# A hybrid decoder layer on one core: the sums of the first channel tile's weights made by adding DMAs, and their high and low parts made beside the output projection

## The chip, the core and the metric

The kernel runs on one core of one Trainium2 chip. The metric is the device time of one execution in microseconds. Before the change three executions took 1217.89, 1218.16 and 1218.32 us; their median is 1218.16 us.

A core has a matrix engine (PE, whose weight loads the profile shows apart as PEld), three engines for elementwise work (DVE, ACT, POOL), a queue that issues most transfers (SP), and 16 DMA engines that carry the transfers out. Each engine runs its own instructions in a fixed order and waits for others by semaphores.

## The reference

What is computed is one decoder layer over 1024 tokens of width 1024, in float32. Cut to its frame:

```
h   = x * (1 + sc1) + sh1                      # the condition c gives six rows: sh, sc, g, twice
fox = forgetting_attention(h @ w_in ...)       # 8 heads of 64, causal softmax with a forget-gate bias
ret = retention(h @ w_in ...)                  # 4 heads of 128, in chunks of 128
x   = layer_norm(ALPHA * x + g1 * (concat(fox, ret) @ w_out), ln1)
h   = x * (1 + sc2) + sh2
u   = causal_depthwise_conv(h @ w_up)          # w_up: 1024 x 5632, width-3 convolution
a, b = split(u)
y   = (gelu(a) * b) @ w_down                   # w_down: 2816 x 1024
x   = layer_norm(ALPHA * x + g2 * y, ln2)
```

## The kernel before

**Float32 by parts.** The matrix engine multiplies a rounded float32 form (fp32r in the profile). So each operand is split into a high part (a cast, on ACT) and a low part (the operand minus its high part, on DVE), and each product is three matmuls: high by high, high by low, low by high.

**The stages, in order of time.** The retention heads and their projections (to about 222 us), the values of the attention heads (to about 273 us), eight attention heads of eight query blocks each (to about 480 us), the output projection `op_mm` over eight tiles of 128 tokens with the first layer norm (to about 575 us), the up-projection with convolution and gate over 22 channel tiles `ff` (to about 1000 us), and the down-projection with the second layer norm.

**Seven products for eight.** The up-projection multiplies 2x2 blocks in Winograd's way: for each channel tile seven products `prod(ff, p)` of sums of weight blocks with sums of input blocks. With `a` and `b` the two weight tiles of channel tile `ff` (loaded by `w_load`, each 128 x 8 x 128, lower half `[0:4]` and upper half `[4:8]`), the weights of the products are: `a` itself (`wA`, products 1 and 2), `b_low + b_high` and that plus `a_low` (`wS`, products 5 and 6, from `w_s`), `a_low + b_low` and `b_high` (`wD`, products 7 and 4, from `w_d`), and `a_high` plus the second half of the `wS` sum (`wZ`, product 3, from `w_4`). The sums are four instructions on DVE (L1217, L1219, L1232, L1240). Then come the high parts on ACT (L1199, L1243) and the low parts on DVE (L1203, L1244). For `ff = 0` all this stands between the last tile of the output projection and the channel loop (L1375 to L1406).

**The inputs of the products** are made at the same place. `h2_turn` transposes each normed tile on PE and writes it to the tiles `hr` by ACT (L910). `h2_low` makes the sums of input blocks on DVE (L937 to L949). `h2_split` makes the parts `t1`, `t2`, `t3`, `t4` (in the profile `ht`; high on ACT L879, low on DVE L883).

**Parking.** During the attention heads `w_out` is split piece by piece: `park_load` loads 128 x 512 floats, `park_high` and `park_low` make the parts on ACT (L990) and DVE (L997), and `park_store` writes them to device memory (`wod`), from where `wo_load` brings them back. There are 16 pieces.

**Adding DMAs.** `add_to` issues on POOL's queue a transfer that adds its source to its destination in device memory. It makes sums for the down-projection during the channel loop. Its destinations are filled beforehand by plain copies within device memory, `down_base` (L1112), during the attention heads.

**What sets the order.** A planner orders the instructions of each engine ahead of time, by their place in the program and by when it reckons their operands and their buffers to be ready. An instruction that is ready in this reckoning goes ahead of an earlier one that is not. On the chip each engine then keeps that order and waits where an operand is late. `tc.issue_after(ins)` puts the instructions of its block that run on the engine of `ins` behind `ins` in that order; it does nothing to other engines. `pins` keeps instructions to be named so.

**Buffers.** On-chip tiles share slots by tag. Those that matter here: X has 16 slots of 4 KB per partition, S 3, R 4, and the small T 4. When the channel loop begins, X holds eight tiles `hr` and the eight tiles of the two inputs `11` and `21`. S holds the second half-tiles of the output projection (`so`) and the gate row `g_row`. Tiles of attention weights (`wqkr`, loaded by `fox_w` at L638 two heads ahead) are in R.

Of the kernel before, what the change touches and what calls it, by code (L numbers as in the profile page):

```python
# [8 lines left out]
F32 = mybir.dt.float32  # L9
F32R = mybir.dt.float32r  # L10
# [5 lines left out]
P = 128  # L16
S = 1024
# [6 lines left out]
NFF = DFF // P  # L24
# [7 lines left out]
def kernel(  # L32
# [23 lines left out]
    nc = tc.nc  # L56
# [10 lines left out]
    def slot(tag, shape, dtype, name, padded=None):  # L67
        return gp.tile(shape, dtype, tag=tag, bufs=NB[tag], name=name, padded_shape=padded)
# [714 lines left out]
    def fox_scores(h, i, T, beside=None):  # L783
        qh, ql, ks, nb = T["qh"], T["ql"], T["ks"], T["nb"]
        span = (i + 1) * P
        tag = "S" if i % 2 == 0 else "R" if h < FH - 1 else "VM"
        Ssb = slot(tag, [P, S], F32, f"S{h}_{i}")
        cuts = [(0, min(max(span, 256), 512))]
        if span > 512:
            cuts.append((512, max(span, 768)))  # L790
        mn = small([P, 1], f"mn{h}_{i}")
        qs = slice(i * P, (i + 1) * P)
        pt = bank2(f"ps{h}_{i}")
        for k0, k1 in cuts:
            last = k0 <= i * P < k1
            nc.tensor.matmul(pt[:, k0:k1], qh[:, qs], ks[:, k0:k1], start=True, stop=False)
            nc.tensor.matmul(pt[:, k0:k1], ql[:, qs], ks[:, k0:k1],
                             start=False, stop=not last)
            if last:
                nc.tensor.matmul(pt[:, i * P:(i + 1) * P], identb, maskb,  # L800
                                 start=False, stop=True)
        pins["min"] = nc.vector.tensor_tensor_reduce(  # L802
            out=Ssb[:, :span], in0=pt[:, :span], in1=nb[:, :span], scale=1.0, scalar=3e38,
            op0=ALU.add, op1=ALU.min, accum_out=mn,
        )
        if beside is not None:
            beside()
        den = small([P, 1], f"dn{h}_{i}")
        pins["exp"] = nc.scalar.activation(  # L809
            Ssb[:, :span], Ssb[:, :span], AF.Exp, scale=-1.0, bias=mn, accum_out=den,  # L810
        )
        nc.vector.reciprocal(den, den)  # L812
        nc.gpsimd.tensor_tensor(  # L813
            out=Ssb[:, :span], in0=Ssb[:, :span], in1=den.to_broadcast([P, span]),
            op=ALU.mult,
        )
        return Ssb
# [152 lines left out]
    def h2_split(key, sl):  # L970
        for c in range(2):
            top_hi(key, c, sl)
            low = top_lo(key, c, sl)
        return low
# [1 line left out]


    wod = [dp.tile([2, P, D], F32, tag=f"wod{m}", name=f"wod{m}") for m in range(ND)]
    PIECES = [(m, slice(n, n + 512)) for m in (4, 5, 6, 7, 0, 1, 2, 3) for n in (0, 512)]
    park, wo = {}, {}  # L980

    def park_load(k):
        if k < len(PIECES):
            m, sl = PIECES[k]
            park[k] = [tmp([P, 512], F32, f"park{k}_{u}") for u in range(2)]
            nc.sync.dma_start(park[k][1], w_out[m * P:(m + 1) * P, sl])

    def park_high(k):
        hi, raw = park[k]
        nc.scalar.copy(hi.bitcast(F32R), raw)  # L990

    def park_low(k):

        if k in park:
            hi, raw = park[k]
            with tc.issue_after(pins["min"].ins):
                nc.vector.tensor_tensor(out=raw.bitcast(F32R), in0=raw, in1=hi, op=ALU.subtract)  # L997

    def park_store(k):
        if k in park:  # L1000
            m, sl = PIECES[k]
            for u, t in enumerate(park.pop(k)):
                nc.sync.dma_start(wod[m][u][:, sl], t)

    def wo_load(m):
        wo[m] = []
# [53 lines left out]
    def op_mm(i, m4):  # L1060
        for n in range(2):
            op_half(i, m4, n)
# [29 lines left out]
    def op_end(i):  # L1092
        for n in range(2):
            op_sum(i, n)
        op_mean(i)
        op_norm(i)
# [8 lines left out]
    def add_to(dst, src):  # L1105
        return nc.gpsimd.dma_start(dst, src, accum_op=ALU.add, max_dma_last_dim=2048)  # L1106

    def down_base(m):
        for q, k in [divmod(v, NK) for v in range(m, 4 * NK, FH)]:
            t, n = ((0, 0), (1, 1), (1, 1), (1, 0))[q]  # L1110
            with tc.issue_after(pins["nb"].ins):
                nc.sync.dma_start(td[q, k], wdq[t, k][:, n * 512:(n + 1) * 512])  # L1112

    LAG = 3
    LOADS = {0: (4, 5), 1: (6, 7), 2: (0, 1), 3: (2, 3)}
    T = {0: fox_alloc(0)}
# [10 lines left out]

    for s_ in range(FH * NT + LAG + 1):
        h, i = divmod(s_, NT)
        if h < FH:  # L1130
            if i == 0:
                if h % 4 == 0:
                    for half in range(2):
                        mixF[h // 4, half] = slot("VM", [P, 2, 512], F32, f"mixF{h // 4}_{half}")
            if i == 3:
                w = nw
                if h + 1 < FH:
                    T[h + 1] = fox_alloc(h + 1)
            if i >= 3:
                proj(h, i)  # L1140
            k, late = divmod(s_ - 4, 3)
            Sb[s_] = fox_scores(h, i, T[h], (lambda: park_low(k - 1)) if late == 1 else None)
            if i == 4 and h + 2 < FH:
                nw = fox_w(h + 2)
            if i == 6:
                down_base(h)
            if late == 0 and k >= 0:
                park_load(k)
            if late == 1:
                park_store(k - 1)  # L1150
            if late == 2 and k in park:
                with tc.issue_after(pins["exp"].ins):
                    park_high(k)
        r = s_ - LAG - 1
        if r >= 0 and r % 2 == 1:
            fox_pv(r // NT, (r % NT) // 2)
        r = s_ - LAG
        if 0 <= r < FH * NT:
            fox_turn(r // NT, r % NT, Sb.pop(r))
        if h < FH and not (i >= 3):  # L1160
            proj(h, i)
        if h == FH - 1 and i == 0:
            for q in range(2):
                op_load(q)
            g_row = slot("S", [P, D], F32, "g_row0")
            nc.sync.dma_start(g_row, bcast_rows(gates[0], D))
        if h == FH - 1:
            for m in LOADS.get(i, ()):
                wo_load(m)
            if i in (2, 3):  # L1170
                op_split(i - 2, 1)
            if i >= NT - 2:
                op_half(0, 1, i - NT + 2)
        if s_ == FH * NT:
            for q in range(2):
                x_load(q)
                sos[q] = slot("X", [P, S], F32, f"so{q}")
        if s_ == FH * NT + 1:
            op_mm(1, 1)
            op_split(0, 0)  # L1180
# [9 lines left out]
    def w_load(ff, u):  # L1190
        if ff < NFF:
            t = slot("R", [P, ND, P], F32, f"w{'ab'[u]}{ff}")
            nc.sync.dma_start(t, w_up[u * NFF + ff])
            (ra, rb)[u][ff] = t
# [27 lines left out]
    def w_s(ff, tag="X"):  # L1222

        if ff < NFF:
            w_s_sums(ff)
            W[ff, 5], W[ff, 6] = w_split(rs[ff], tag, f"wS{ff}")

    def w_d(ff, tag="X"):

        if ff < NFF:  # L1230
            a, b = ra[ff], rb[ff]
            nc.vector.tensor_tensor(out=b[:, 0:4, :], in0=a[:, 0:4, :], in1=b[:, 0:4, :],  # L1232
                op=ALU.add)
            W[ff, 7], W[ff, 4] = w_split(b, tag, f"wD{ff}")
# [125 lines left out]


    for i in range(NT - 1):
        op_mm(i, 0)
        op_split(i + 1, 0)
        if i + 2 < NT:
            x_load(i + 2)
            op_load(i + 2)
            op_split(i + 2, 1)
        op_end(i)
        if i > 0:  # L1370
            h2_turn(i - 1)
            h2_low(i - 1)
            op_mm(i + 1, 1)

    w_load(0, 0)  # L1375
    w_load(0, 1)
    w_load(1, 0)
    with tc.issue_after(pins["norm"].ins):
        w_a(0, "VM")
# [10 lines left out]
    with tc.issue_after(pins["norm"].ins), tc.issue_after(pins["bias"].ins):  # L1390
        h2_split("t1", slice(0, 3 * P))
        up_12(0)
        w_s(0, "S")
        h2_turn(NT - 1)
        h2_low(NT - 1)
        for key in ("t2", "t1"):
            low = h2_split(key, slice(3 * P, 4 * P))
        up_65(0, 0)
        with tc.issue_after(low.ins):
            up_12(1)  # L1400
        w_d(0)
        h2_split("t3", slice(0, 4 * P))
        h2_split("t4", slice(0, 4 * P))
        w_4(0)
    w_load(1, 1)
    w_load(2, 0)  # L1406

    for ff in range(NFF):
        up_657(ff)
        w_s(ff + 1)  # L1410
        w_d(ff + 1)
        w_load(ff + 2, 1)
        if ff + 2 == NFF:
            w_4(ff + 1)
        if ff > 0:
            up_12(ff + 1)
        if ff + 2 < NFF:
            w_a(ff + 2)
        up_43(ff)
        if ff + 2 < NFF:  # L1420
            w_4(ff + 1)
        w_load(ff + 3, 0)
        geglu(ff)
# [312 lines left out]
```

## Time and profile before

| what | value |
|---|---|
| median of three executions | 1218.16 us |
| the profiled execution, its own time | 1220.08 us |
| its span, first to last instruction | 1218.4 us |
| granted clock of the matrix engine, mean | 0.998 |
| DVE busy, share of the span | 910.4 us, 75% |
| ACT busy, share of the span | 653.1 us, 54% |
| POOL busy, share of the span | 229.1 us, 19% |
| moved by DMA, mean | 178 GB/s |

A span is what one profiled execution shows from its first to its last instruction; 1.7 us of the execution lie around it. Times of day in the views are microseconds from the start of the span. Rows of a timeline read: start, length, engine, line, operation, output and inputs, count, and in brackets how long the engine sat idle before it and what ended that. Rows of a table by windows read: the window, its length, then for PE, PEld, DVE, ACT and POOL the busy time and the number of instructions, then the granted clock, the share of the DMA engines and GB/s.

### The profile page before, as it was taken

Reading aid. Unit: us, or ns where it says so; the run is one execution under the profiler, and the core shown is the slowest. Engines: PE = TensorE matmul, PEld = TensorE weight load, DVE = VectorE, ACT = ScalarE, POOL = GpSimd, SP = SyncE. Lnnn points to the kernel's source line nnn. Section 1 sums busy time; section 2 is a strip of 40 time slices with the busy share of each in tenths; the row PEclk is TensorE's granted clock in tenths of the full one; section 3 lists DMA queues with packets and bytes.
Section 4 is the critical chain, followed back from the end, with each engine's and each line's share of the span. In section 5 each row is a group of like instructions: output and inputs, shape, how many; then the busy total and the mean of one; then the engine's idle time right before and its main releaser. Section 6 shows DMA issues by size and latency. Waiting matters only on the chain.

```text
span 1218.4 us, 17192 instructions
## 1 busy us (share of the span) xinstructions
PE 1199.6 (98%) x6005; PEld 1002.2 (82%) x6005; DVE 910.4 (75%) x1757; ACT 653.1 (54%) x1201; POOL 229.1 (19%) x274
## 2 busy tenths in 40 slices
PE   8999999999999999999999999999999999999997
PEld 6788888998888888888888888888888878888885
DVE  7847747766788887456988778787787775876596
ACT  6635445346777776567754545445454554544452
POOL 0015335013323333000021323211100010000021
PEclk9999999999999999999999999999999999999999
DMA  9524444604575558223268887776454588966751
GB/s 357 226 87 123 138 154 135 205 29 147 167 238 169 185 189 335 95 75 117 87 177 208 191 220 187 173 188 175 141 138 130 154 250 270 331 216 199 260 178 69
DMA packets 94278, 216.56 MB, mean 178 GB/s; under 512 B 10784, under 2 KB 17136, under 8 KB 94192
## 3 DMA queue, kind: packets, MB, share of 16 engines
q1 hardware_dynamic: 81520, 192.40, 45.7%
q0 software_dynamic: 12672, 23.07, 11.8%
q8 instruction: 47, 0.77, 0.3%
q14 instruction: 39, 0.32, 0.1%
HBM read 173.45 MB, written 76.59 MB: 205 GB/s over the span
## 4 chain that ended last, share of the span: by engine, by line
PE 88%; DMA 5%; DVE 3%; ACT 2%; issue 1%; SPq 0%; DVEq 0%; ACTq 0%
PE rp L152 11%; PE dX L1477 10%; PE dZ L1477 7%; PE uX L1260 6%; PE uX L1259 6%; PE uX L1261 6%; PE uY L1261 5%; PE uY L1259 5%; PE uY L1260 5%; PE vp L152 4%; DMA ada<-in_ada_dram 3%; PE pv L851 3%; PE op L189 2%; PE op L191 2%; PE op L190 2%; PE pt L835 2%
## 5 line engine op out<-in xcount | busy, mean ns | idle before, releaser
L152 PE MATMUL rp<-wr,hhi 128*128 128x512 f32 x400 | 127.9, 401 | 0.0
L1454 ACT CAST dh<-dr 128x1024 fp32r<-128x1024 f32 x66 | 67.6, 1050 | 77.9 <-DMA dr<-td 31.7
L1466 DVE TENSOR_TENSOR dl<-dr,dh 128x1024 fp32r<-128x1024 f32 x66 | 80.1, 1237 | 37.5 <-ACT dh L1454 37.2
L813 POOL TENSOR_TENSOR S<-S,dn 128x128 f32<-128x128 f32 (+3 forms) x64 | 73.6, 1154 | 152.8 <-DVE dn L812 126.0
L1106 POOL DMA_DIRECT2D sd<-gd x22 | 18.1, 823 | 399.8 <-DMA sd<-y 233.3
L152 PEld LDWEIGHTS rp<-wr,hhi 128*128 128x128 f32 x400 | 71.6, 189 | 12.7
L152 PE MATMUL rp<-wr,hlo 128*128 128x512 f32 x200 | 78.6, 393 | 0.0
L1477 PE MATMUL dX<-dh 128*128 128x512 f32 x176 | 68.5, 389 | 0.0
L1477 PE MATMUL dX<-dl,dh 128*128 128x512 f32 x176 | 68.5, 389 | 0.0
L1477 PE MATMUL dX<-dh,dl 128*128 128x512 f32 x176 | 68.5, 389 | 0.0
L1274 ACT COPY u<-uX 128x512 f32<-128x512 f32 x44 | 25.7, 585 | 69.1 <-PE uX L1261 69.1
L152 DVE CUSTOM_DVE_ANT_0 ada<-ada,csb,bcol 128x1024 f32<-128x1024 f32 x46 | 60.1, 1309 | 3.5 <-DMA ada<-in_ada_dram 3.5
L842 DVE TENSOR_TENSOR pt<-pt,pt 128x512 fp32r<-128x512 f32 (+2 forms) x96 | 50.6, 549 | 10.7 <-ACT pt L841 9.2
L809 ACT ACTIVATE S<-S,mn 128x128 f32<-128x128 f32 (+3 forms) x64 | 49.9, 780 | 13.6 <-DVE mn L802 13.0
L765 PE MATMUL qk<-hhi,wqh 128*128 128x512 f32 x128 | 55.1, 430 | 0.0
L802 DVE CUSTOM_DVE_ANT_0 S<-ps,nb 128x128 f32<-128x128 f32 (+3 forms) x64 | 47.5, 742 | 6.1 <-PE ps L800 5.2
L841 ACT CAST pt<-pt 128x512 fp32r<-128x512 f32 (+2 forms) x96 | 43.9, 479 | 14.5 <-PE pt L835 13.6
L1477 PE MATMUL dZ<-dh 128*128 128x512 f32 x132 | 51.6, 391 | 0.0
L767 PE MATMUL qk<-hhi,wql 128*128 128x512 f32 x128 | 51.5, 402 | 0.0
L1477 PE MATMUL dZ<-dl,dh 128*128 128x512 f32 x132 | 51.4, 389 | 0.0
L1477 PE MATMUL dZ<-dh,dl 128*128 128x512 f32 x132 | 51.4, 389 | 0.0
L189 PE MATMUL op<-wo,mxs 128*128 128x512 f32 x128 | 51.1, 399 | 0.0
(1048 smaller groups left out, 3655.0 us busy)
## 6 DMA issues: line engine op xcount, KB each, us to landing
ada<-in_ada_dram SPq DMA_DIRECT2D x48, 512.0 KB, 3.8
td<-in_w_down_dram SPq DMA_DIRECT2D x44, 256.0 KB, 5.9
wa<-in_w_up_dram SPq DMA_DIRECT2D x22, 512.0 KB, 4.8
wb<-in_w_up_dram SPq DMA_DIRECT2D x22, 512.0 KB, 4.2
gd<-y SPq DMA_DIRECT2D x22, 512.0 KB, 3.2
sd<-y SPq DMA_DIRECT2D x44, 256.0 KB, 3.4
dr<-sd SPq DMA_DIRECT2D x44, 256.0 KB, 4.2
dr<-td SPq DMA_DIRECT2D x44, 256.0 KB, 4.5
```

The source lines that it names most:

```text
L152: order[key] = fn(*args, **kw)
L189: mm(pt, ahi, whi, start=start, stop=False)
L765: nc.tensor.matmul(pt, whi[:, j, :], hhi[j][:, sl], start=(j == 0), stop=False)
L767: nc.tensor.matmul(pt, wlo[:, j, :], hhi[j][:, sl], start=False, stop=(j == ND - 1))
L813: nc.gpsimd.tensor_tensor(out=Ssb[:, :span], in0=Ssb[:, :span], in1=den.to_broadcast([P, span]), op=ALU.mult,)
L842: nc.vector.tensor_tensor(out=dl, in0=src, in1=f(dh), op=ALU.subtract)
L1259: nc.tensor.matmul(pt, whi, bh, start=start, stop=False, skip_group_check=True)
L1260: nc.tensor.matmul(pt, whi, bl, start=False, stop=False, skip_group_check=True)
L1261: nc.tensor.matmul(pt, wlo, bh, start=False, stop=stop, skip_group_check=True)
L1454: nc.scalar.copy(hi, raw)
L1466: nc.vector.tensor_tensor(out=lo, in0=raw, in1=f(hi), op=ALU.subtract)
L1477: nc.tensor.matmul(pt, w_[:, 0, q], m_[:, 1, :], start=start and n_ == 0, stop=stop and n_ == 2, skip_group_check=True)
```

## The change

The weight sums of channel tile 0 are no longer made by `w_s(0)`, `w_d(0)` and `w_4(0)`. There are four steps in their place.

1. `up_base`, called in the fifth attention head at its third block, copies four half-tiles of `w_up` (128 x 512 floats each) to new tiles `usum` in device memory, by four transfers on SP's queue, behind the load of that head's bias row (`pins["nb"]`).
2. `up_adds`, called before the first product of the output projection, issues four adding DMAs on POOL, behind POOL's last product of the attention heads (`pins["pool"]`, L813). The third reads what the first made, the fourth what the third made.
3. Five more pieces are parked, one in each of the first five tiles of the output projection: the upper half of `b`, which needs no sum, and the four sums. Their high parts stand behind the norm of the next tile on ACT, their low parts behind its second sum on DVE. Both parts are stored to new tiles `upd`.
4. `up_parts` loads the parts where `w_s(0)`, `w_d(0)` and `w_4(0)` stood: two tiles of 512 KB in S (`wS0`), two of 512 KB in X (`wD0`), two of 256 KB in S (`wZ0`).

The load of the whole tile `b` of channel tile 0, `w_load(0, 1)`, falls away. The DVE instructions of `w_s(1)` are put behind the last low part of `t4`. The matmuls are the same.

```diff
@@ fox_scores
-        nc.gpsimd.tensor_tensor(
+        pins["pool"] = nc.gpsimd.tensor_tensor(
@@ parking
-    PIECES = [(m, slice(n, n + 512)) for m in (4, 5, 6, 7, 0, 1, 2, 3) for n in (0, 512)]
+    PIECES = [(w_out[m * P:(m + 1) * P, n:n + 512], [wod[m][u][:, n:n + 512] for u in range(2)])
+              for m in (4, 5, 6, 7, 0, 1, 2, 3) for n in (0, 512)]
...
-    def park_low(k):
+    def park_low(k, behind="min"):
...
@@ before the head loop
+    ua0, ub0 = [[w_up[u * NFF][:, k:k + 4, :] for k in (0, 4)] for u in range(2)]
+    usum = [dp.tile([P, 4, P], F32, tag=f"usum{k}", name=f"usum{k}") for k in range(4)]
...
+    NW = len(PIECES)
+    for n, src in ((3, ub0[1]), (0, usum[0]), (1, usum[1]), (2, usum[2]), (4, usum[3])):
+        PIECES.append((flat(src), [flat(upd[2 * (n // 2) + u][:, n % 2]) for u in range(2)]))
+
+    def up_base():
+        for k, src in ((0, ub0[0]), (1, ua0[0]), (2, ua0[0]), (3, ua0[1])):
+            with tc.issue_after(pins["nb"].ins):
+                nc.sync.dma_start(usum[k], src)
+
+    def up_adds():
+        for k, src in ((0, ub0[1]), (2, ub0[0]), (1, usum[0]), (3, usum[1])):
+            with tc.issue_after(pins["pool"].ins):
+                add_to(flat(usum[k]), flat(src))
+
+    def up_parts(n, tag, name):
+        out = []
+        for u, c in enumerate("hl"):
+            t = slot(tag, [P, 8 if n < 2 else 4, P], F32, f"{name}{c}")
+            nc.sync.dma_start(t, upd[2 * n + u].rearrange("p t k c -> p (t k) c"))
+            out.append(t.bitcast(F32R))
+        return [tuple(t[:, k:k + 4, :] for t in out) for k in ((0, 4) if n < 2 else (0,))]
@@ head loop
+            if (h, i) == (4, 2):
+                up_base()
-            if late == 0 and k >= 0:
+            if late == 0 and 0 <= k < NW:
                 park_load(k)
@@ output projection
     for i in range(NT - 1):
+        if i == 0:
+            up_adds()
+        park_load(NW + i)
         op_mm(i, 0)
...
         op_end(i)
+        if NW + i - 1 in park:
+            with tc.issue_after(pins["norm"].ins):
+                park_high(NW + i - 1)
+            park_low(NW + i - 1, "sum")
+            park_store(NW + i - 1)
...
-    w_load(0, 1)
...
-        w_s(0, "S")
+        W[0, 5], W[0, 6] = up_parts(0, "S", "wS0")
...
-        w_d(0)
+        W[0, 7], W[0, 4] = up_parts(1, "X", "wD0")
         h2_split("t3", slice(0, 4 * P))
-        h2_split("t4", slice(0, 4 * P))
-        w_4(0)
+        end = h2_split("t4", slice(0, 4 * P))
+        W[0, 3] = up_parts(2, "S", "wZ0")[0]
...
     for ff in range(NFF):
         up_657(ff)
-        w_s(ff + 1)
+        if ff == 0:
+            with tc.issue_after(end.ins):
+                w_s(ff + 1)
+        else:
+            w_s(ff + 1)
```

More of the change, by code (lines that the diff above doesn't have):

```diff
@@ L983, in park_load @@
         if k < len(PIECES):
-            m, sl = PIECES[k]
             park[k] = [tmp([P, 512], F32, f"park{k}_{u}") for u in range(2)]
-            nc.sync.dma_start(park[k][1], w_out[m * P:(m + 1) * P, sl])
+            nc.sync.dma_start(park[k][1], PIECES[k][0])
     def park_high(k):
@@ L990, in park_high @@
         nc.scalar.copy(hi.bitcast(F32R), raw)
-    def park_low(k):
+    def park_low(k, behind="min"):
         if k in park:
             hi, raw = park[k]
-            with tc.issue_after(pins["min"].ins):
+            with tc.issue_after(pins[behind].ins):
                 nc.vector.tensor_tensor(out=raw.bitcast(F32R), in0=raw, in1=hi, op=ALU.subtract)
@@ L1000, in park_store @@
         if k in park:
-            m, sl = PIECES[k]
-            for u, t in enumerate(park.pop(k)):
-                nc.sync.dma_start(wod[m][u][:, sl], t)
+            for dst, t in zip(PIECES[k][1], park.pop(k)):
+                nc.sync.dma_start(dst, t)
     def wo_load(m):
@@ L1112, in down_base @@
                 nc.sync.dma_start(td[q, k], wdq[t, k][:, n * 512:(n + 1) * 512])
+    ua0, ub0 = [[w_up[u * NFF][:, k:k + 4, :] for k in (0, 4)] for u in range(2)]
+    usum = [dp.tile([P, 4, P], F32, tag=f"usum{k}", name=f"usum{k}") for k in range(4)]
+    upd = [dp.tile([P, 2 if k < 2 else 1, 4, P], F32, tag=f"upd{k}_{u}", name=f"upd{k}_{u}")
+           for k in range(3) for u in range(2)]
+    NW = len(PIECES)
+    flat = lambda t: t.rearrange("p k c -> p (k c)")
+    for n, src in ((3, ub0[1]), (0, usum[0]), (1, usum[1]), (2, usum[2]), (4, usum[3])):
[15 more added lines that the diff above has]
+        return [tuple(t[:, k:k + 4, :] for t in out) for k in ((0, 4) if n < 2 else (0,))]
     LAG = 3
```

## The prediction

> **What bounds the kernel now.** I read the page first, for the busy shares and the chain that ended last.
>
> ```profile
> PE 1199.6 (98%) x6005; PEld 1002.2 (82%) x6005; DVE 910.4 (75%) x1757; ACT 653.1 (54%) x1201; POOL 229.1 (19%) x274
> ...
> PE 88%; DMA 5%; DVE 3%; ACT 2%; issue 1%; SPq 0%; DVEq 0%; ACTq 0%
> ```
>
> The matrix engine is busy for 98% of the span and carries 88% of the chain. The change leaves every matmul as it is, so it can gain only where PE stands still. Next I asked the table by windows around the place that the change empties, and the waits of PE from 500 to 610 us.
>
> ```profile
> 520.00:530.00 10.00, 10.00 (x50) 8.35 (x49) 4.46 (x11) 5.21 (x14) 0.00 (x0) 1.00 0.22 80
> ...
> 590.00:600.00 10.00, 9.10 (x51) 7.74 (x50) 9.85 (x14) 6.12 (x8) 0.00 (x0) 1.00 0.16 52
> 600.00:610.00 10.00, 10.00 (x45) 8.27 (x45) 10.00 (x12) 7.29 (x9) 0.00 (x0) 1.00 0.35 107
> ```
> ```profile
> PE uX L1260 <- DVE ht L883: 0.9, 1, 0.9
> ```
>
> Between 500 and 610 us PE waits once, 0.9 us, for DVE, and DVE is full there (9.85 of 10). PE's own timeline has the wait, and the chain has what stands before it.
>
> ```profile
> 592.76 0.28 PE L1261 MATMUL uY<-ht,wS0l 128*128 128x256 f32 x1
> 592.88 0.46 PE L1259 MATMUL uX<-ht,wD0h 128*128 128x512 f32 x1
> 594.24 0.50 PE L1260 MATMUL uX<-ht,wD0h 128*128 128x512 f32 x1 [0.90 <-DVE ht L883]
> 594.58 0.40 PE L1261 MATMUL uX<-ht,wD0l 128*128 128x512 f32 x1
> 594.81 0.39 PE L1259 MATMUL uX<-ht,wD0h 128*128 128x512 f32 x1
> ```
> ```profile
> 589.18 1.66 ACT ht L879 x3
> 590.84 0.96 ACT wD0h L1199
> 591.83 1.23 DVE wD0l L1203
> 593.05 1.15 DVE ht L883
> ```
>
> Matmuls of 512 columns start 0.23 us apart (594.58 to 594.81). From 592.88 to 594.24 are 1.36 us, so 1.13 are lost, and 0.11 more at the restart (594.24 to 594.58). **1.24 us is all that this place can give**: 0.1% of the time. The cause is as the change assumes: the low part of `t3` stands behind the split of `wD0`, ACT then DVE, and both go away.
>
> [...]
>
> **The change, part by part.** *Off DVE and ACT at the transition.*
>
> ```profile
> 580.25 0.69 DVE L1217 TENSOR_TENSOR ws<-wb 128x512 f32<-128x512 f32 x1
> ...
> 582.18 0.68 DVE L1240 TENSOR_TENSOR wa<-wa,ws 128x512 f32<-128x512 f32 x1
> ...
> 584.25 1.22 DVE L1203 TENSOR_TENSOR wS0l<-ws,wS0h 128x1024 fp32r<-128x1024 f32 x1
> ...
> 589.68 1.43 DVE L883 TENSOR_TENSOR ht<-hr,ht 128x256 fp32r<-128x256 f32 x4
> ...
> 595.24 0.68 DVE L1244 TENSOR_TENSOR wZ<-wa,wZ 128x512 fp32r<-128x512 f32 x1
> ```
> ```profile
> 582.71 1.05 ACT L1199 CAST wS0h<-ws 128x1024 fp32r<-128x1024 f32 x1
> 583.66 0.83 ACT L879 CAST ht<-hr 128x768 fp32r<-128x768 f32 x1
> 584.39 2.90 ACT L910 ACTIVATE hr<-nT,AB 128x128 f32<-128x128 f32 x8
> ```
>
> Four sums (0.69 each, the first and the last are shown), 1.22, 1.23 and 0.68 leave DVE: 5.9 us. ACT loses two casts of 1.05 and the half cast of `wZ`, some 2.6 us. The low part of `t3` then follows the four small `ht` (they end at 591.1) at once and, with 1.15 us, is out by 592.3, before PE asks. The wait for DVE goes. What is late next is the transfers that take its place.
>
> *`wD0` in X.* X is full with `hr` and the two inputs until the first small `ht` has read its `hr`: 589.68 plus a quarter of 1.43 is 590.04. Both loads of `wD0` stand behind such a release. It comes earlier by what leaves ACT ahead of the eight `hr` of 584.39, the cast of `wS0` (0.95 from start to start): about 589.1, and 589.4 for the second slot.
>
> ```profile
> so<-mixR SPq DMA_DIRECT2D x5, 256.0 KB, 2.8
> wb<-in_w_up_dram SPq DMA_DIRECT2D x2, 512.0 KB, 3.5
> ```
> ```profile
> DMA to landing us min/median/max: 3.4/4.7/9.1
> ```
>
> The first two rows are transfers of 480 to 600 us (KB each, median us to landing); the third is of all weight loads, L1193. With 3.5 us `wD0h` lands at 592.6 and `wD0l` at 592.9, or up to 0.8 later because the two share the engines (an estimate: half of the 1.7 us that 512 KB take at the 312 GB/s of a row below). PE asks for the high part at 592.88 and for the low one two matmuls later, at 593.33. So the new wait is 0 to 0.4 us with 3.5 us of landing, 0.9 to 1.6 with 4.7, and over 5 with 9.1. Traffic is low there (a share of 0.16), so I take the near rows: **0.3 us**. [...]
>
> *`wZ0` in S.* S has three slots for the four tiles of `wS0` and `wZ0`. The low part of `wZ0` must wait until PE has used `wS0`: 592.76 plus 0.28. With 2.8 us it lands at 595.9. PE asks for it after the twelve matmuls of product 7 (593.1 plus 12 x 0.23) and two of product 3, at 596.3. Product 4 cannot be pulled ahead, since DVE must first read the same bank. I take **0.1 us**, with bounds 0 and, at the 4.7 us of a weight load, 1.4. `wS0` itself takes the slots that the last squares and sums of the projection leave, ahead of the norm of the last tile, and costs nothing.
>
> *The adding DMAs* go to an engine with nothing to do: POOL ends its last product at 481.3 and is idle until the channel loop. How long an adding DMA takes is in the row of L1106.
>
> ```profile
> 479.40 1.90 POOL L813 TENSOR_TENSOR S<-S,dn 128x1024 f32<-128x1024 f32 x1 [1.72 <-DVE dn L812]
> ```
> ```profile
> DMA to landing us min/median/max: 4.0/6.0/11.7
> ```
>
> Three in a chain take 18 us at the median, 35 at most: done by 500 or 517. The sums are wanted one per tile of 48 matmuls (11 us), the first a tile after the projection begins, the last of the chain three tiles after that. Cost 0; were the first late by a tile, SP would hold up one `so` load.
>
> *Parking beside the projection.* Five casts and five subtractions, by the rows of the sixteen pieces of before:
>
> ```profile
> L990 ACT CAST park<-park x16: 603/607/632, 297.6 to 445.2; 128x512 fp32r<-128x512 f32 x16
> L997 DVE TENSOR_TENSOR park<-park,park x16: 679/690/1164, 301.1 to 449.6; 128x512 fp32r<-128x512 f32 x16
> ```
>
> That is 0.6 us of ACT and 0.7 of DVE in each of five tiles. PE covers both. The tightest tile is the fifth, where DVE also makes the first sums of input blocks:
>
> ```profile
> 546.79 1.25 ACT L1089 ACTIVATE acc<-acc,onm,ors 128x1024 f32<-128x1024 f32 x1 [1.63 <-DVE onm L1088]
> ```
> ```profile
> 550.51 1.04 PE L902 MATMUL nT<-ident,acc 128*128 128x128 f32 x8
> ```
>
> Its norm ends 2.5 us before PE turns the tile, and the added cast stands behind the norm, so it does not hold it. Behind the cast on ACT wait only casts for the next tile's products, which a pass of 24 matmuls (5.4 us) separates from PE. SP gets a load and two stores per tile; behind the stores stands the next `so` load, whose slot comes free only with the next tile's square, some 10 us later. Cost 0; without that cover 0.7 us per tile, 3.5 in all.
>
> *`up_base` in the heads.* Four transfers of 256 KB at 0.6 us of SP each, in the one stretch where SP and the DMA engines are full:
>
> ```profile
> 358.71 1.83 SPq L1112 DMA_DIRECT2D td<-in_w_down_dram  x3
> 360.65 0.52 SPq L638 DMA_DIRECT2D wqkr<-in_w_qk_dram  x1
> 361.22 0.43 SPq L986 DMA_DIRECT2D park<-in_w_out_dram  x1
> 366.48 0.33 SPq L1003 DMA_DIRECT2D wod<-park  x1
> ```
> ```profile
> 360.65 7.30 DMA wqkr<-in_w_qk_dram
> 367.97 1.06 ACT wqh L641
> ```
> ```profile
> 360.00:365.00 5.00, 5.00 (x34) 4.22 (x33) 4.54 (x10) 2.86 (x5) 0.00 (x0) 1.00 0.99 312
> ```
> ```profile
> 376.48 0.63 PE L835 MATMUL pt<-ident,S 128*128 128x128 f32 x4 [0.74 <-DVE ks L777]
> ```
>
> The bias row of the fifth head goes out before all this; the copies of `td` behind it come first, being earlier in the program. SP is then free from 361.65 to 366.48. There four issues of 0.6 us fit, and behind them wait only a store, a bias row for a later head and more copies. At that place I take **0.2 us** for their traffic (1 MB at 312 GB/s, 3.4 us of full DMA). The bounds are 0 and 3.4.
>
> **The sum** is -1.24 + 0.3 + 0.1 + 0.2 = -0.6 us: 1219.5 for the profiled execution's 1220.08, and 1217.6 against the median of 1218.16. A measurement of this kernel can tell about 0.2%, 2.4 us, from no change, and this is a quarter of that.
>
> **The rivals.** *The wait only changes its name.* Loads that can start only when a slot comes free land 4.7 us later, not 3.5: 1.2 us for `wD0`, up to 0.7 for `wZ0`, and the fox stretch as above. That gives back 1.2 to 1.9 for 1.24: 1218.2 to 1219.0. For it speaks that the slots are freed by the very chain that sets the wait; against it the low traffic. The change would then not do what it says.
>
> *Slower: `up_base` goes ahead of the weights of head 5.* `wqkr` at 360.65 waits for a slot, and copies from later in the program (three of them in the row) were let past it. Copies from device memory to device memory wait for no slot, so four more may pass if the planner saw SP idle there. Each puts 256 KB at 312 GB/s, 0.84 us, ahead of a load that ACT uses the moment it lands, and PE's 0.74 us at 376 lie on the chain behind it. The transition's own gain is 0.84 (1.24 less 0.3 and 0.1), so one passing eats it and the second makes the kernel slower. With all four it is 1217.3 + 3.4 = 1220.7, which alone can be measured. Against it: `wqkr` follows the sixth copy at once.
>
> [...]
>
> **How the numbers follow.** Forecast 0.57 (1216.9 to 1218.2). The wait renamed 0.17. `up_base` ahead 0.20, half of it beyond 0.2%. Room in PE, or a luckier order of the heads, 0.03. Another order of the heads or of SP in the projection that costs over 2.4 us, 0.03. So faster by over 0.2%: 0.03; slower: 0.10 + 0.03 = 0.13; within: 0.84. The range goes from 1216.7, where the transition gives everything (1216.9, less 0.2 for the spread of the runs), to 1220.9, all four copies ahead and the same spread.
>
> **What would show it.** Right: PE's wait for DVE `ht` in 590 to 600 us is gone and at most 0.6 us of waits for transfers `wD0` or `wZ0` stand there; PE is 9.4 or more of 10; no PE wait appears in 500 to 580; `wqkr` of head 5 still leaves before the four copies. Wrong: a wait of ACT for `wqkr` longer than 0.8 us with PE idle behind it, waits of ACT for `so` in the projection, or PE waiting over 1.2 us at the transition.

## The result, and the profile after

The changed kernel takes **1221.62 us** (median of nine executions, 1220.42 to 1223.19) against 1218.09 us of the kernel before, run beside it (1217.51 to 1219.65). The ratio is 1.0024 with a 95% interval of 1.0015 to 1.0032: slower by some 3 us. In a later comparison with the kernel before (1218.75 us) it was 1220.44 us, ratio 1.0015 (1.0002 to 1.0029). The profiled execution took 1223.19 us, its span is 1221.5 us. The prediction was 1217.6 us, with a range up to 1220.9.

The place that the change was made for did get better. The table by windows of the changed kernel (columns as before: window, length, busy time and count of PE, PEld, DVE, ACT, POOL, clock, DMA share, GB/s):

```profile
590.00:600.00 10.00, 9.87 (x54) 8.13 (x53) 9.75 (x18) 6.88 (x12) 0.00 (x0) 1.00 0.40 131
```

PE is busy 9.87 of 10 us where it was 9.10, and its wait of 0.9 us for DVE is gone. What is left there are waits of PEld, in its waits from 500 to 620 us:

```profile
PEld uX L1288 <- issue: 0.3, 1, 0.3
PEld uX L1290 <- DMA wD0l<-upd: 0.3, 1, 0.3
PEld uY L1288 <- ACT u L1303: 0.3, 1, 0.3
```

The loss is 220 us earlier. SP's timeline of the changed kernel (start, length, queue, line, operation):

```profile
358.83 1.83 SPq L1111 DMA_DIRECT2D td<-in_w_down_dram  x3
360.70 1.88 SPq L1126 DMA_DIRECT2D usum<-in_w_up_dram  x3
362.70 0.52 SPq L638 DMA_DIRECT2D wqkr<-in_w_qk_dram  x1
...
366.86 0.50 SPq L1126 DMA_DIRECT2D usum<-in_w_up_dram  x1
```

Three of the four copies of `up_base` stand ahead of the load `wqkr`, which leaves at 362.70 instead of 360.65. The row of its issue (KB, us from issue to landing) shows that it also takes 8.1 us to land, where it took 7.3:

```profile
wqkr<-in_w_qk_dram SPq DMA_DIRECT2D x1, 512.0 KB, 8.1
```

So the weights are there 2.9 us later. How that reaches PE is read from three timelines of the changed kernel, ACT, then DVE, then PE:

```profile
370.86 1.05 ACT L641 CAST wqh<-wqkr 128x1024 fp32r<-128x1024 f32 x1 [2.98 <-DMA wqkr<-in_w_qk_dram]
371.81 0.83 ACT L809 ACTIVATE S<-S,mn 128x640 f32<-128x640 f32 x1
372.55 0.18 ACT L809 ACTIVATION_READ_ACCUMULATOR S<-S,mn 128x1 f32 x1
372.75 0.36 ACT L857 COPY mixF<-pv 64x256 f32<-64x256 f32 x1
```
```profile
371.94 1.29 DVE L644 TENSOR_TENSOR wql<-wqkr,wqh 128x512 fp32r<-128x512 f32 x2 [3.38 <-ACT wqh L641]
...
373.23 0.94 DVE L802 CUSTOM_DVE_ANT_0 S<-ps,nb 128x768 f32<-128x768 f32 x1
...
374.09 1.17 DVE L997 TENSOR_TENSOR park<-park,park 128x512 fp32r<-128x512 f32 x1
375.28 0.43 DVE L858 TENSOR_TENSOR mixF<-pv,mixF 64x256 f32<-64x256 f32 x1
```
```profile
372.58 0.61 PE L835 MATMUL pt<-ident,S 128*128 128x128 f32 x4
375.77 0.50 PE L765 MATMUL qk<-hhi,wqh 128*128 128x512 f32 x1 [2.58 <-DVE mixF L858]
```

The cast `wqh` is for a later head, and PE does not need it yet. But ACT and DVE keep their order, and behind the waiting cast stand the softmax and the `mixF` of the head that PE is working on. `mixF` reads a bank of PE's output, and PE cannot start the next product before that bank is free. PE stands still for 2.58 us. In the kernel before, the same `mixF` on DVE and the product behind it on PE stood here:

```profile
372.40 0.43 DVE L858 TENSOR_TENSOR mixF<-pv,mixF 64x256 f32<-64x256 f32 x1
```
```profile
372.94 0.47 PE L765 MATMUL qk<-hhi,wqh 128*128 128x512 f32 x1
```

From 372.40 to 375.28 are 2.88 us; PE had some 0.3 us in hand.

There is a second part, in the table by windows of the changed kernel behind the pause:

```profile
375.00:376.00 1.00, 0.23 (x1) 0.23 (x2) 0.85 (x4) 0.97 (x4) 0.00 (x0) 1.00 0.22 82
376.00:377.00 1.00, 1.00 (x5) 0.76 (x5) 0.97 (x4) 0.95 (x3) 0.69 (x1) 0.85 0.78 274
377.00:378.00 1.00, 1.00 (x4) 0.81 (x3) 1.00 (x3) 0.64 (x2) 0.77 (x1) 0.50 0.97 197
378.00:379.00 1.00, 1.00 (x4) 0.70 (x3) 0.97 (x2) 1.00 (x3) 0.00 (x0) 0.50 0.85 193
379.00:380.00 1.00, 1.00 (x5) 0.58 (x4) 0.94 (x4) 0.58 (x2) 0.11 (x1) 0.50 0.94 281
```

The clock falls to 0.50 at 376.7 us and stays there for 3.4 us, a little into the window from 380 us. PE is fully busy there and does four matmuls in a microsecond, some 0.43 us from start to start instead of 0.23. No such row stands in the trace of before between 360 and 390 us.

To compare runs by place, the text below uses PE's **excess**: for every matmul the time from its start to the next one's, less the lower quartile of that time for matmuls of the same shape in the kernel before, added up in slices of 20 us. It counts pauses, slow clock and late starts alike.

| slice, us | before | changed | changed, again |
|---|---|---|---|
| 360 to 380 | 1.7 | 5.0 | 4.7 |
| 480 to 580, five slices | 0.6, 0.3, 0.1, 0.1, 0.3 | 0.7, 0.3, 0.1, 0.1, 0.3 | 0.7, 0.3, 0.1, 0.1, 0.3 |
| 580 to 600 | 1.5 | 0.8 | 0.7 |
| 980 to 1000 | 2.8 | 2.8 | 1.0 |

So +3.3 us at 360 and -0.7 at 580, each read from one profiled execution, and that of the changed kernel is the slowest of its nine, so its 3.3 us lie at the upper end. The last row shows why single executions aren't compared by their span: the same kernel has 2.8 us there in one execution and 1.0 in another.

### The profile page after: what moved, and what is told of

It is laid out like the page before. It is cut to its first block, busy times and chain, and to the rows that moved or that the text cites. A ratio compares the mean times of both kernels' runs of the same rounds, so it can differ in the third digit from the quotient of the medians.

```text
span 1221.5 us, 17266 instructions
## 1 busy us (share of the span) xinstructions
PE 1202.0 (98%) x6005; PEld 1003.5 (82%) x6005; DVE 909.0 (74%) x1755; ACT 653.3 (53%) x1203; POOL 232.1 (19%) x278
## 4 chain that ended last, share of the span: by engine, by line
PE 72%; DMA 11%; DVE 9%; ACT 4%; issue 3%; SPq 1%; DVEq 0%; ACTq 0%
PE rp L152 11%; PE uX L1288 6%; PE uX L1289 6%; PE uX L1290 6%; PE uY L1290 4%; PE uY L1288 4%; PE uY L1289 4%; PE vp L152 4%; PE pv L851 3%; DVE dl L1506 3%; DMA dr<-in_w_down_dram 3%; DMA ada<-in_ada_dram 3%; PE dX L1517 2%; PE op L189 2%; PE op L191 2%
## 5 line engine op out<-in xcount | busy, mean ns | idle before, releaser
L813 POOL TENSOR_TENSOR S<-S,dn 128x128 f32<-128x128 f32 (+3 forms) x64 | 73.6, 1154 | 156.3 <-DVE dn L812 132.9
L766 PE MATMUL qk<-hlo,wqh 128*128 128x512 f32 x128 | 51.1, 399 | 0.0
```

What stands on the lines that cost most here:

```text
L766: nc.tensor.matmul(pt, whi[:, j, :], hlo[j][:, sl], start=False, stop=False)
L813: pins["pool"] = nc.gpsimd.tensor_tensor(out=Ssb[:, :span], in0=Ssb[:, :span], in1=den.to_broadcast([P, span]), op=ALU.mult,)
```

## The experiments

**T1**: the loss is the order on SP, copies ahead of `wqkr`. **T2**: the loss is the megabyte of extra traffic in that stretch, wherever it stands. **T3**: part of it comes from the parking, the adding DMAs or the new loads. The time of each run is given with its ratio to the kernel before, run in the same comparison.

**The copies behind the load** (x1_behind).

```diff
-        nc.sync.dma_start(raw, w_qk[h])
+        pins["wq"] = nc.sync.dma_start(raw, w_qk[h])
...
-            with tc.issue_after(pins["nb"].ins):
+            with tc.issue_after(pins["wq"].ins):
                 nc.sync.dma_start(usum[k], src)
```

> The changed kernel with one thing moved: the four copies of up_base stand on SP behind the load of wqkr for the head two further on, instead of three of them ahead of it. T1 (the loss is the order: the load leaves 2.05 us later and lands 2.9 us later): the excess of PE at 360 to 380 us goes back from 5.0 us to about 1.7, ACT's wait for wqkr from 2.98 us to at most 0.8, and the time is 1218.1 less the 0.7 us that PE gained at the transition, 1217.4 us (1216.9 to 1218.0), ratio to the kernel before 0.9994. T2 (the loss is the 1 MB of traffic, wherever in this stretch it stands): 2 to 3 us stay, 1220 to 1221.5 us, ratio 1.002.

Measured: 1217.58 us, ratio 0.9995 (0.9987 to 1.0004). SP's timeline of this run:

```profile
360.46 0.52 SPq L639 DMA_DIRECT2D wqkr<-in_w_qk_dram  x1
...
366.35 2.42 SPq L1126 DMA_DIRECT2D usum<-in_w_up_dram  x4
```

ACT's wait for `wqkr` is 0.68 us, the excess at 360 us is 2.2, at 580 us still 0.8. T1 holds and T2 falls: the same four transfers of 256 KB, three of them over 5 us later, leave 0.5 us of the 3.3 (0.9 to 1.1 us in three later runs with this order).

**The copies alone** (x2_copies_alone): the kernel before, and in it `usum`, `up_base` and its call.

```diff
+            if (h, i) == (4, 2):
+                up_base()
```

> The kernel before with the four copies of up_base added at their place in the change and nothing else; nothing reads what they write. T1 (all of the loss comes from these copies): 1218.1 + 3.3 = 1221.4 us (1220.8 to 1222.2), ratio 1.0027, with ACT waiting about 3 us for wqkr and PE losing about 5 us instead of 1.7 at 360 to 380 us. T3 (a part of the loss comes from the parking in the projection, the adding DMAs or the loads at the transition): less than 1220.3 us.

Measured: 1221.12 us, ratio 1.0017 (1.0008 to 1.0026). SP puts three copies ahead here too, `wqkr` leaves at 363.42, and the waits from 340 to 400 us have

```profile
ACT wqh L641 <- DMA wqkr<-in_w_qk_dram: 4.3, 1, 4.3
...
PE qk L765 <- DVE mixF L858: 3.9, 1, 3.9
```

The excess at 360 us is 5.7, at 580 us 1.6 as before. The copies alone make the whole loss: T1 again. By the excess nothing is left for T3. (That the load leaves 0.7 us later than in the changed kernel is not the work of the order: in this execution SP's row of `td` ahead of the copies begins 0.4 us later and the three issues take 2.19 us for 1.88.)

**A quarter of the bytes** (x3_quarter_copies): as the last run, 64 KB for each copy.

```diff
-                nc.sync.dma_start(usum[k], src)
+                nc.sync.dma_start(usum[k][:, 0:1, :], src[:, 0:1, :])
```

> As the run before, but each of the four copies moves 64 KB instead of 256 KB, so their bytes fall from 1 MB to 0.25 MB while SP still issues four transfers. If the price is SP's time to issue (0.6 us each ahead of wqkr): wqkr still leaves about 2 us late, PE loses about 2 to 2.5 us, 1220.1 to 1220.6 us. If the price is the bytes ahead of the load (0.84 us for 256 KB): a quarter of it is left, 1218.7 to 1219.0 us.

Measured: 1219.4 us, ratio 1.0006 (0.9997 to 1.0015), between the two. All four small copies went ahead, 2.52 us of SP, so `wqkr` left later than in any other run (363.84). But it landed in 6.4 us, not 8.1 or 8.3, and ACT waited 2.86 us. So both parts of the price are real: the issues decide when the load leaves, and with a quarter of the bytes around it the load landed 1.9 us sooner than in the run before. The excess at 360 us is 4.3. The time lies between the two ranges that were expected, 1218.7 to 1219.0 for the bytes and 1220.1 to 1220.6 for the issues, and in neither; it doesn't size the parts.

**One copy ahead, and two** (x4_one_ahead, x8_two_ahead).

```diff
-            with tc.issue_after(pins["wq"].ins):
+            with tc.issue_after(pins["nb" if k == 0 else "wq"].ins):
```

(for two, `k < 2`).

> The changed kernel with one copy of up_base ahead of wqkr and three behind it. T1 (each copy ahead of the load costs its issue of 0.6 us and some of its traffic): about 1 us more than the run with all four behind, about 1218.4 us (1218.0 to 1218.9), ACT's wait for wqkr near 1 us. T2 (traffic wherever it stands): the same as the run with all four behind, both at 1220 us or more.

> Two copies of up_base ahead of wqkr and two behind. By issue times wqkr leaves 1.2 us later than with none, about 361.6 us, and with 7.5 us of landing ACT starts its cast at about 369.1 us, some 1.1 to 1.5 us after it is free (one copy: no wait; three: 3.0 us). T1: PE's excess at 360 to 380 us is 2.5 to 3.5 us, the time 1218.4 to 1219.3 us. If the price were the same for each copy, the one copy would already have cost 1.1 us; so a step from 1.6 us to 5.0 us at the second or third copy is expected rather than a line. T2 (traffic wherever it stands): as with none, 1217.6 us.

Measured: one ahead 1217.86 us, ratio 1.0001 (0.9992 to 1.0010), with no wait of ACT for `wqkr` at all; two ahead 1220.28 us, ratio 1.0015 (1.0005 to 1.0025), and its time is above what was expected though its excess is in place. (The kernel before beside it took 1218.94 us, and 1218.18 beside the first four runs.) The runs in order of dose:

| run | copies ahead | `wqkr` leaves | lands after | ACT waits for it | PE's pause before `qk` | excess at 360 us |
|---|---|---|---|---|---|---|
| before | none made | 360.65 | 7.3 | 0 | 0 | 1.7 |
| x1_behind | 0 of 4 | 360.46 | 7.6 | 0.7 | 0.3 | 2.2 |
| x4_one_ahead | 1 | 360.95 | 6.6 | 0 | 0 | 1.6 |
| x8_two_ahead | 2 | 361.84 | 7.8 | 2.0 | 1.6 | 3.5 |
| changed | 3 | 362.70 | 8.1 | 3.0 | 2.6 | 5.0 |
| x2_copies_alone | 3 | 363.42 | 8.3 | 4.3 | 3.9 | 5.7 |
| x3_quarter_copies | 4, 64 KB each | 363.84 | 6.4 | 2.9 | 2.5 | 4.3 |

The price is not the same for each copy. ACT's wait for `wqkr` costs PE nothing up to about 0.4 us, and beyond that PE's pause is ACT's wait less some 0.3 to 0.4 us. Four runs below, which are not in the table, lie on the same line: waits of 0.4, 1.1, 1.1 and 1.2 us and pauses of 0, 0.7, 0.8 and 0.8. One copy ahead stays within what is free, so the expectation of 1 us for it was wrong. The rows of the table are one execution each, and `wqkr` left at 360.5 to 361.1 us in the five runs with no copy ahead of it, so a difference of half a microsecond between two rows says little.

How long the load takes to land isn't a matter of the bytes ahead of it alone: 7.3 to 7.7 us with no copy ahead, 6.6 and 6.9 with one, 7.8 with two, 7.3 to 8.3 with three. Why it landed sooner with one copy ahead than with none wasn't settled.

**Everything made, nothing used** (x9_made_not_used): copies behind `wqkr`, adding DMAs and parking as in the change; channel tile 0 by `w_s(0)`, `w_d(0)`, `w_4(0)` as before.

```diff
+    w_load(0, 1)
...
-        W[0, 5], W[0, 6] = up_parts(0, "S", "wS0")
+        w_s(0, "S")
...
-        W[0, 7], W[0, 4] = up_parts(1, "X", "wD0")
+        w_d(0)
...
-        W[0, 3] = up_parts(2, "S", "wZ0")[0]
+        w_4(0)
```

> The kernel before with the copies (behind wqkr), the adding DMAs, the five parked pieces and their stores, but channel tile 0 still makes its sums and parts on DVE and ACT, and the stored parts are not read. If the adding DMAs and the parking beside the projection cost nothing: 1218.2 us (1217.8 to 1218.7), ratio 1.000, PE's excess at 480 to 580 us as before (0.6, 0.3, 0.1, 0.1, 0.3 in slices of 20 us) and 1.5 us at 580 to 600. If each parked piece costs its 0.7 us on the path: 1221.7 us. With the gain of 0.7 us at the transition taken away, this run and the one with the copies behind (1217.6 us) differ by that gain alone.

Measured: 1218.48 us, ratio 0.9996 (0.9987 to 1.0006). The excess from 480 to 580 us is 0.5, 0.3, 0.1, 0.1, 0.3, and 1.5 at 580. A row of its table by windows:

```profile
540.00:560.00 20.00, 20.00 (x94) 16.62 (x93) 16.47 (x41) 16.12 (x39) 0.00 (x0) 1.00 0.38 136
```

PE is full. The adding DMAs and the parking cost nothing that can be seen, and the 1.5 against 0.8 us at 580 is the gain of using the stored parts, 0.7 us. Only the traces show this gain: by their ratios, 0.9996 and 0.9995, the times of this run and of the one with the copies behind can't be told apart.

**The loads of `wD0` earlier** (x7_early_half, then x10_swapped_slots). In the run with the copies behind, PEld waits 0.32 us at 592.63 ahead of product 7 and 0.30 us for `wD0l` at 593.79:

```profile
592.63 0.19 PEld L1288 LDWEIGHTS uX<-ht,wD0h 128*128 128x128 f32 x1 [0.32 <-issue]
...
593.79 0.19 PEld L1290 LDWEIGHTS uX<-ht,wD0l 128*128 128x128 f32 x1 [0.30 <-DMA wD0l<-upd]
```

```diff
-            t = slot(tag, [P, 8 if n < 2 else 4, P], F32, f"{name}{c}")
+            t = slot(tag[u], [P, 8 if n < 2 else 4, P], F32, f"{name}{c}")
...
-        W[0, 7], W[0, 4] = up_parts(1, "X", "wD0")
+        W[0, 7], W[0, 4] = up_parts(1, "RX", "wD0")
```

> The run with the four copies behind wqkr, and the high parts wD0h in R, whose slot the dropped tile b of channel tile 0 leaves free, instead of X. If the loads of wD0 into X are what is still late at the transition (PEld waits 0.3 us before the first matmul of product 7 and 0.3 us for wD0l, together about 0.5 us of PE): the excess of PE at 580 to 600 us falls from 0.8 to about 0.3 us, and the time is 0.5 us below the run with the copies behind, about 1217.1 us (1216.5 to 1217.6), ratio 0.9991. If the wait before product 7 is instead for the inputs t3 or for the accumulators, nothing changes: 0.8 us and 1217.6 us. A loss would show as PE waiting for the weight sums of channel tile 1 at 600 to 615 us, because ws of tile 1 comes into R after one more tile.

Measured: 1219.85 us, ratio 1.0008 (0.9999 to 1.0017). The excess at 580 us falls from 0.8 to 0.1, as expected of the loads. But at 600 us it rises from 0.1 to 2.3, and DVE's timeline of this run says why:

```profile
599.61 0.69 DVE L1246 TENSOR_TENSOR ws<-wb 128x512 f32<-128x512 f32 x1 [3.16 <-PE uX L1289]
```

`ws` of channel tile 1 took the slot of `wD0h` and waited until PE had used it; the expectation had named that loss. The second try exchanges two tiles instead:

```diff
-        W[0, 7], W[0, 4] = up_parts(1, "RX", "wD0")
+        W[0, 7], W[0, 4] = up_parts(1, "SX", "wD0")
...
-        W[0, 3] = up_parts(2, "SS", "wZ0")[0]
+        W[0, 3] = up_parts(2, "XS", "wZ0")[0]
```

> The run with the four copies behind wqkr, with two tiles of channel tile 0 exchanged: the high parts wD0h take the third slot of S, which is free early, and the high parts wZ0h, half as big and wanted later, the second slot of X; ws of channel tile 1 keeps its slot in R. If the two loads of wD0 into X were what is late, PE's excess at 580 to 600 us is 0.1 to 0.3 us, as with wD0h in R, and 600 to 620 stays at 0.1 instead of 2.3: 0.5 us below the run with the copies behind, ratio to the kernel before 0.9990 to 0.9995. If the loss at 600 to 620 in the run before came from the early loads and not from the slot of ws, it stays: ratio 1.0005 or more.

> The same, with one copy of up_base ahead of wqkr and three behind, as in the run with one ahead. PE's excess at 360 to 380 us 1.6 to 2.2 us with ACT's wait for wqkr under 0.8 us, at 580 to 600 us 0.1 to 0.3 us. 1217.0 us (1216.4 to 1217.8), ratio to the kernel before 0.9988 to 0.9996.

Measured: 1217.40 us, ratio 0.9991 (0.9982 to 1.0000), and with one copy ahead 1217.32 us, ratio 0.9992 (0.9983 to 1.0000). The excess at 580 us is 0.2 and 0.1, at 600 us 0.1 in both. PE of the second run goes through the transition without a gap:

```profile
592.27 0.28 PE L1290 MATMUL uY<-ht,wS0l 128*128 128x256 f32 x1
592.39 0.40 PE L1288 MATMUL uX<-ht,wD0h 128*128 128x512 f32 x1
592.62 0.40 PE L1289 MATMUL uX<-ht,wD0h 128*128 128x512 f32 x1
```

These two are below the kernel before by 1.5 us at the median (1218.88 in their comparison), with an interval that just reaches 1. They have the lowest ratios of the versions run and are clearly below the changed kernel, but by time they can't be told from the run with the copies behind alone (0.9995, 0.9987 to 1.0004).

**The clock behind the pause** (x12_shorter_pause, after_again).

```diff
-            for kb in kbs:
+            for kb in [*kbs] * (2 if (h, i, t) == (3, 3, 0) else 1):
                 nc.tensor.transpose(
```

> The changed kernel, in which the four transposes of PE ahead of the long pause at 373 us are made twice, so that PE stands still some 0.3 us less there while the load of wqkr is as late as before. In the traces the granted clock fell to 0.50 for 3 us after pauses of 2.58 and 3.89 us and stayed at 1.00 after one of 2.45 us. If the clock follows the length of the pause: a pause of about 2.3 us, no slice from 375 to 382 us under 0.99, and 1.2 to 1.5 us less lost than in the changed kernel, about 1220.3 us, although ACT's wait for wqkr stays near 3 us. If the fall of the clock has nothing to do with the pause: it is there again and the time is that of the changed kernel. The planner also moves some products of the next head, which may shift either by some tenths.

> The changed kernel once more, on the same chip: ACT's wait for wqkr about 3 us, PE's pause 2.5 to 2.7 us, and, if the fall of the clock belongs to a pause of that length, again 0.50 for about 3 us behind it; 1221.6 us (1220.8 to 1222.4), ratio 1.0015 to 1.0032. If the clock stays at 1.00 at the same pause, the fall depends on more than the length of the pause.

Measured, with the pause shortened: 1219.73 us, ratio 1.0008 (0.9999 to 1.0018); the changed kernel beside it 1220.44 us, ratio 1.0015 (1.0002 to 1.0029). By time alone the two can't be told apart. The traces can. With the pause shortened, ACT still waits 2.6 us for `wqkr`, PE starts again at the same time, and the clock stays:

```profile
372.22 1.04 PE L835 MATMUL pt<-ident,S 128*128 128x128 f32 x8
375.00 0.50 PE L765 MATMUL qk<-hhi,wqh 128*128 128x512 f32 x1 [1.73 <-DVE mixF L858]
...
378.60 0.63 PE L835 MATMUL pt<-ident,S 128*128 128x128 f32 x4 [0.79 <-DVE ks L777]
```

In the changed kernel, run again, the pause is 2.41 us, the restart at 375.02, and the same transposes come at 379.47:

```profile
375.02 0.50 PE L765 MATMUL qk<-hhi,wqh 128*128 128x512 f32 x1 [2.41 <-DVE mixF L858]
...
379.47 0.60 PE L835 MATMUL pt<-ident,S 128*128 128x128 f32 x4
```

379.47 less 378.60 is 0.87 us, but not all of that is the price of the slow clock: in the changed kernel one product of the next head (0.31 us) stands ahead of these transposes, which here comes behind them. That leaves some 0.6 us. The excess, 4.7 against 3.8, can't be taken for it either, since 0.7 us of the difference is the pause that the doubled transposes fill. A run without them gives the same price: with the quarter copies the pause is 2.45 us, as long as here, the clock stays, and the excess is 4.3 against 4.7. So the slow clock costs some 0.4 to 0.6 us of the loss. Six matmuls at 0.43 us for 0.23 are 1.2 us by themselves; a part is hidden, since at full speed PE waits 0.79 us for `ks` right behind. The expected 1.2 to 1.5 was too much, and the pause shrank by 0.7 us, not 0.3.

## Why the prediction was wrong

**The step that failed is `up_base`.** "SP is then free from 361.65 to 366.48. There four issues of 0.6 us fit" took SP's free time on the chip for the place where the planner would put them. The planner works with its own reckoning of when `wqkr` may start, and by it three copies must have been ready sooner; no run shows the reckoning itself, only the order that came of it. The sign was in the rows quoted: three copies of `td`, later in the program, already stood ahead of that load. The run with the copies behind `wqkr` is the order that the forecast assumed: it gave 1217.58 us for the forecast's 1217.6. That this is so near is in part luck, since two terms of the sum were off, as said below.

**The rival was right in mechanism and named its place**, "`up_base` goes ahead of the weights of head 5", but had too low a chance, and its price was too small. It counted 0.84 us of traffic for each copy, 2.5 us for three; the excess rose by 3.3. Left out were SP's own 0.6 us for each issue, which delay the load, and the slow clock, some 0.5 us. The sign that it named, a wait of ACT for `wqkr` longer than 0.8 us with PE idle behind it, is what the trace shows (2.98 us). That all four "alone can be measured" was wrong: three give 1.0024, two 1.0015.

**The 0.2 us for copies that stand behind the load** was low: the excess at 360 us is 2.2 with them (2.6 to 2.8 in three other runs of that order) against 1.7, so 0.5 to 1.1 us. Its bounds, 0 and 3.4, hold it.

**The 1.24 us at the transition** were right: PE's wait for DVE is gone, and with the loads early too the excess falls from 1.5 to 0.1 or 0.2. **The 0.3 us for the loads of `wD0`** were mis-sized, about 0.6 (0.8 less 0.1 or 0.2). `wD0l` took 4.5 us to land in the run with the copies behind, where it went out 0.4 us behind `wD0h`, and with `wD0h` in R, where it went out alone at 589.28, PEld took it at 593.05 without a wait, at most 3.8 us later; the forecast took 3.5 and had named 0.8 us more as possible. **The 0.1 us for `wZ0`** did not show. The net at the transition was forecast as 0.84 us of gain and is 0.7.

**Room in PE**, to which the chances give 0.03 together with a luckier order of the heads, is shown by no run: the lowest median is 1217.32 us, and at 600 to 610 us PEld is busy for 8.29 of 10 us in the changed kernel, where it was 8.27.

**Cost 0 for the adding DMAs and the parking** was right, by the run in which all is made and nothing used. In the changed kernel the adding DMAs land after 4.8 us (sources that are inputs) and 5.6 us (sources just made), medians of two each, where 6.0 was assumed.

## What to carry to other kernels

A transfer that is added "in a free stretch" goes where the planner reckons it ready, not where the queue looks free; if a load that others wait for stands near, say the order explicitly, and look for copies that already pass it. A late load holds up engines that don't use it where its first user stands ahead of unrelated work in an engine's order: here ACT waited 2.98 us for weights of a later head, and PE stood still for 2.58 us on the current one. A pause of PE cost more than its length here: behind one of 2.41 us the clock stood at 0.50 for 3.41 us, which cost some 0.4 to 0.6 us more. What moved work gains at its destination has to be set against what its preparation costs at its source, which may be hundreds of microseconds earlier.

## What the runs showed of the hardware

In the midst of the program the granted clock fell to 0.50 in four of the thirteen traces: the changed kernel (at 376.71 us), the changed kernel again (375.92), the copies alone (377.75) and the run with `wD0h` in R (998.99). Each time it stayed there for 3.41 us and was then back at 1.00. It also fell behind PE's last matmul: that ends at 1213.24 us in the changed kernel, and the clock falls at 1216.39; in the kernel before it ends at 1209.75 us, and the clock falls at 1214.3.

The length of the pause alone doesn't decide. The clock fell behind pauses of 2.41, 2.58 and 3.89 us; it stayed at 1.00 behind pauses of 2.45, 1.73 and 1.6 us. PE's busy time was read as well. These are the 3.41 us ahead of the fall and the 3.41 us behind it, in the changed kernel again and in the run with `wD0h` in R:

```profile
372.51:375.92 3.41, 1.00 (x5) 0.77 (x5) 3.23 (x9) 2.78 (x6) 1.62 (x2) 1.00 0.65 218
375.92:379.34 3.42, 3.42 (x11) 2.41 (x10) 3.33 (x8) 2.52 (x5) 1.30 (x2) 0.50 0.83 220
```
```profile
995.57:998.99 3.42, 1.65 (x8) 1.05 (x7) 2.61 (x4) 1.72 (x2) 0.00 (x0) 1.00 0.25 100
998.99:1002.40 3.41, 3.41 (x10) 2.63 (x9) 2.09 (x2) 0.00 (x0) 0.81 (x1) 0.50 0.85 311
```

PE was busy for 1.00 and 1.65 us of the stretch ahead, which leaves 2.41 and 1.77 us in which it stood still; in the changed kernel it was 0.94 us and in the run of the copies alone 1.15. With the shortened pause a stretch of this length shows hardly more than the 1.65, and the clock stayed at 1.00:

```profile
373.14:376.55 3.41, 1.68 (x9) 1.29 (x8) 3.23 (x9) 3.04 (x6) 1.81 (x2) 1.00 0.54 178
```

With the quarter copies the clock stayed at 1.00 too, though PE is busy for at most 0.96 us of any 3.41 us that hold the whole pause of 2.45 us (an estimate: 3.41 less 2.45). So neither the length of the pause nor this busy time tells the pauses with a slow clock behind them from the others. What decided was not shown, and no run was made to test it.
